# Hybrid SSD and MLA layer: attention output normalized in three calls of the chunk loop, fixed conv rows, later reciprocal and group norm, five gate buffers

## The chip, the cores and the metric

The kernel runs on one core of a Trainium2 chip. The engines named here are TensorE (PE, with its weight loads PEld), VectorE (DVE), ScalarE (ACT), GpSimd (POOL) and SyncE (SP, which here only issues DMAs). The metric is the device time of one execution in microseconds, as the median of several runs.

## What is computed

A decoder layer over a sequence of 1024 positions and 1024 channels, in float32. Two branches read the same normalized input; the gated branches are summed and go through a projection and a gated MLP.

```python
h = rms_norm(x, norm_mix_g)
z, xbc, dt_raw, q_a, kv_a, k_rope_raw, gates = split(h @ w_in)
y_ssd = ssd_mixer(z, xbc, dt_raw, ...) @ w_ssd_proj
y_mla = mla_mixer(q_a, kv_a, k_rope_raw, ...) @ w_mla_proj
g_ssd, g_mla = split(sigmoid(gates + gate_b), 2)
x = x + (g_ssd * y_ssd + g_mla * y_mla) @ w_o
u_gate, u_val = split(causal_depthwise_conv(rms_norm(x, norm_ffn_g) @ w_up, conv_ffn_w, conv_ffn_b), 2)
x = x + (silu(u_gate) * u_val) @ w_down

# ssd_mixer: 4 groups of 8 heads, state 128, chunks of 128 positions
xs, bm, cm = split(silu(causal_depthwise_conv(xbc, conv_w, conv_b)))
y = ssd_chunked_scan(xs * dt, dt * a, bm, cm) + xs * d_skip
y = rms_norm((y * silu(z)).reshape(b, l, 4, 512), norm_g)     # per group
# mla_mixer: 16 heads, causal softmax attention, output 64 wide per head
```

## The kernel before

Float32 matmuls with a wide right side are done as three passes over split operands: `split` writes a high part `hi` (on ACT) and a rest `lo` (on DVE or POOL), and `mm3` (L149 to L151) multiplies hi by hi, hi by lo and lo by hi. Weights come through `load_w`: two DMAs on SP into `wraw` (two buffers of 128 x 512), a cast to `whi` on ACT (L127), a subtraction to `wlo` on POOL (L128; `w_eng` sets the engine). A step is one such triple of 128 x 512 matmuls, and a tile of a projection takes 16 steps into the two PSUM banks `lin`.

The order on PE is the order of the code. Every other engine's order is set by the tile framework's scheduler, which simulates the program and lays instructions by when it expects them to be ready; each engine and each DMA queue then runs its own list strictly in order. A tile name with `bufs=n` is a ring of n buffers, and the next writer of a buffer waits for the last user of it, which may be a DMA that stores it.

After the attention (head sums in `l_d`, unnormalized output in `at_d`, both in HBM) the program goes on so:

1. `flush()` finishes the z gates still in the background (`z_tiles`), then the reciprocal of all head sums is made: load `l_d`, one vector instruction, store.
2. `conv_group(0)`: six tiles of `conv_tile`. Each takes 16 steps on PE, copies to a row `craw` on ACT with three zeros ahead of it (a memset on POOL for each new row), one scaled copy on ACT (L768), three shifted multiply-adds on DVE (L770), then tanh (L774) and a last product (L775) in `silu`.
3. The chunk loop over groups 0 to 3, 23 steps `u` each (`ssd_steps`): transposes `xp`, state update `sn` and `st`, outputs `yp`, gating, squares (`ssd_squares`, ACT then POOL). Between the steps `advance` puts background matmuls on PE: the next group's convolutions, z tiles, and for group 3 the MLA projection (`mla_tiles`).
4. Within it `ssd_finish` does the group norm of a half sequence: sums over partitions as matmuls by a column of ones (`np_`, L901), a reciprocal square root by bit trick and three Newton steps (twelve instructions of four columns on DVE), a broadcast of the root on PE (`np_`, L908), four products (L911) and stores to `y_d`.
5. `normalize(n)`, called every third step, 16 times with work: stores the product of the call before, loads a tile of `at_d` and, by two partition broadcasts, the reciprocals from `l_d` (both into `rb`, three buffers) and multiplies on POOL (L937).
6. `mla_tiles` for group 3: per half tile a load of the sigmoid gate from `g_d` into `rb`, 8 steps on PE, one product (L953), a store to `m_d`. Attention output is reloaded by `load_at` into `rb` or `lt` and split.

Of the kernel before, what the change touches and what calls it, by code (L numbers as in the profile page):

```python
# [72 lines left out]
def tile_hybrid_layer(ctx: ExitStack, tc: tile.TileContext, x, cols, cons, w_main, w_small, w_uq, w_ukv,  # L73
# [39 lines left out]
    def rsqrt_mean(dst, ss, n):  # L113

        w = dst.shape[1]
        v = const.tile([P, 32], F32, name="rsv", bufs=1)[:, 0:w]
        a = const.tile([P, 32], F32, name="rsa", bufs=1)[:, 0:w]
        V.tensor_scalar(v, ss, 1.0 / n, EPS, op0=ALU.mult, op1=ALU.add)
        V.tensor_scalar(dst.bitcast(I32), v.bitcast(I32), 1, None, op0=ALU.logical_shift_right)
        V.tensor_scalar(dst.bitcast(I32), dst.bitcast(I32), -1.0, float(0x5F3759DF), op0=ALU.mult, op1=ALU.add)  # L120
        for _ in range(3):
            V.scalar_tensor_tensor(a, dst, -0.5, v, op0=ALU.mult, op1=ALU.mult)
            V.tensor_tensor(a, a, dst, op=ALU.mult)
            V.scalar_tensor_tensor(dst, a, 1.5, dst, op0=ALU.add, op1=ALU.mult)

# [362 lines left out]
    with tc.tile_pool(name="cp", bufs=2) as cp, tc.tile_pool(name="pss", bufs=4, space=PSUM) as pss, \  # L488
# [235 lines left out]
        lv = l_d.rearrange("h (c t) -> (h c) t", t=P)  # L724
        ls = cp.tile([P, 512], F32, name="e", bufs=6)[:, 0:P]
        nc.sync.dma_start(out=ls, in_=lv)
        V.reciprocal(ls, ls)
        nc.sync.dma_start(out=lv, in_=ls)
# [5 lines left out]
    with tc.tile_pool(name="dp", bufs=2) as dp, tc.tile_pool(name="psx", bufs=1, space=PSUM) as psx, \  # L734
# [4 lines left out]
        abcs, zts = [], []  # L739

# [17 lines left out]
        def conv_tile(ct, c):  # L758
            w = load_w(w_main[16 + ct], [P, KD, P])
            raw = dp.tile([P, T + 3], F32, name="craw")  # L760
            G.memset(raw[:, 0:3], 0.0)
            cw = CG_CONVW + 4 * ct
            for half in range(2):
                ps = lin_tile()
                yield from steps([w], h[half], ps, range(KD), KD)
                S.copy(raw[:, 3 + half * 512:3 + half * 512 + 512], ps)
                later()
            S.activation(c, raw[:, 3:T + 3], AF.Identity, bias=col(CG_CONVB + ct), scale=col(cw + 3))  # L768
            for k in range(3):
                V.scalar_tensor_tensor(c, raw[:, k:k + T], col(cw + k), c, op0=ALU.mult, op1=ALU.add)  # L770

            def silu():
                th = raw[:, 0:T]
                S.activation(th, c, AF.Tanh, scale=0.5)  # L774
                V.scalar_tensor_tensor(c, th, 1.0, c, op0=ALU.add, op1=ALU.mult)  # L775

            pend.append(silu)
# [50 lines left out]
        def ssd_state(g, c, inp, st):  # L828
# [4 lines left out]
            nst = dp.tile([P, 512], F32, name="st", bufs=3)  # L833
# [30 lines left out]
        sums = {}  # L864

        def ssd_squares(g, c):
# [5 lines left out]
            G.tensor_tensor(sums[g, c // 4][:, (c % 4) * P:(c % 4 + 1) * P], sq[:, 0, :], sq[:, 1, :], op=ALU.add)  # L872

# [20 lines left out]
        def ssd_finish(g, half):  # L894

            x, s = chan[g], hs_(half)
            if half:
                ssd_squares(g, NT - 1)
            np_ = psy.tile([P, 512], F32, name="np_")
# [4 lines left out]
            rsqrt_mean(rr, np_[:, 0:4], 512)  # L904
            yield
# [18 lines left out]
        stores = []  # L924

        def normalize(n):

            if stores:
                nc.sync.dma_start(out=stores[0][0], in_=stores[0][1])
                stores.pop()  # L930
            if n < 16:
                k, s = n // 2, hs_(n % 2)
                raw, rb = [dp.tile([P, 512], F32, name="rb", bufs=3) for _ in range(2)]
# [3 lines left out]
                G.tensor_tensor(raw, raw, rb, op=ALU.mult)  # L937
                stores.append((at_d[k * P:(k + 1) * P, s], raw))

        def mla_tiles():  # L940
# [3 lines left out]
            def one(w, ct, half):  # L944
                s = hs_(half)
                gt = dp.tile([P, 512], F32, name="rb", bufs=3)
# [35 lines left out]
        drain([conv_group(0)])  # L982
# [4 lines left out]
        for g in range(GROUPS):  # L987
# [7 lines left out]
            for u, _ in enumerate(ssd_steps(g)):  # L995
                advance((u + 1) * n // 23 - u * n // 23)
                if u % 2 and fins and next(fins[0], 0) == 0:
                    fins.pop(0)
                if u % 3 == 1 and (g < 2 or g == 2 and u == 1):
                    normalize(8 * g + u // 3)  # L1000
                if u == 12:
# [551 lines left out]
```

## Time and profile before

| | us |
|---|---|
| median of 3 runs | 2295.05 |
| the runs | 2286.06, 2295.05, 2298.89 |
| the profiled execution | 2296.51 |
| its span, first to last instruction | 2294.4 |
| PE busy | 2205.7 |
| DVE busy | 1430.9 |
| ACT busy | 1014.1 |
| POOL busy | 755.5 |

The profiled execution is one run of the program with the trace on; its span leaves out 2.1 us at its ends. Busy times are sums over the instructions of an engine. Where an engine idles, the trace tells which event ended the idle time, read from semaphores; the engine that made the event may itself have waited. Waits are told per stretch of the span: the z gates and the first convolutions stand at about 711 to 850 us, groups 0 to 2 of the chunk loop at 850 to 1190, group 3 with the MLA projection at 1190 to 1340.

### The profile page before, as it was taken

To read this page: it belongs to the slowest core of one execution; us is meant where nothing else is said; L and a number is where in the kernel's file an instruction comes from. 1 tells how busy PE (TensorE), PEld (TensorE's weight loads), DVE (VectorE), ACT (ScalarE), POOL (GpSimd) and SP (SyncE) were. 2 spreads that over 40 slices of the span, in tenths; PEclk is the share of its full clock that TensorE was granted. 3 is DMA by queue.
4 is the path that set the end of the run, shared out by engine and by line. 5 is a ranking of instruction groups with operands and counts; after the bars stand their busy time and mean duration, and the time that the engine had idled before them with its cause. 6 is when DMAs were issued, how large, how long until landed. Compare 5 with 4: busy or idle time off the path is not lost. (4 is left out here: it accounts for less than half of the span.)

```text
span 2294.4 us, 31427 instructions
## 1 busy us (share of the span) xinstructions
PE 2205.7 (96%) x11488; PEld 1769.3 (77%) x11488; DVE 1430.9 (62%) x2496; ACT 1014.1 (44%) x1852; POOL 755.5 (33%) x821
## 2 busy tenths in 40 slices
PE   8999999999998879999998999999989999999999
PEld 7877777777776667777876778989778888888887
DVE  4566565667662348887876755645887767774432
ACT  5454454454543226565654423424544444443221
POOL 2244432444333444343423310003175555510000
PEclk9999999999999999999999999999999999999999
DMA  3111111111113542545356685543122222227541
GB/s 141 57 66 48 48 42 52 53 48 41 54 48 117 168 147 75 126 104 124 97 156 189 170 280 197 178 144 116 55 92 83 83 83 83 83 101 269 189 148 65
DMA packets 158906, 253.57 MB, mean 111 GB/s; under 512 B 13504, under 2 KB 68480, under 8 KB 158752
## 3 DMA queue, kind: packets, MB, share of 16 engines
q1 hardware_dynamic: 101232, 214.73, 27.2%
q10 hardware_dynamic: 57520, 36.84, 6.8%
q8 instruction: 90, 1.47, 0.3%
q14 instruction: 64, 0.52, 0.1%
HBM read 194.63 MB, written 56.89 MB: 110 GB/s over the span
## 5 line engine op out<-in xcount | busy, mean ns | idle before, releaser
L149 PE MATMUL lin<-h,whi 128*128 128x512 f32 x1440 | 601.1, 417 | 16.4 <-ACT whi L127 10.5
L151 PE MATMUL lin<-h,wlo 128*128 128x512 f32 x1440 | 570.2, 396 | 16.9 <-POOL wlo L128 15.9
L150 PE MATMUL lin<-h,whi 128*128 128x512 f32 x1440 | 568.2, 395 | 0.0
L149 PEld LDWEIGHTS lin<-h,whi 128*128 128x128 f32 x1440 | 274.3, 191 | 124.0 <-issue 57.0
L151 PEld LDWEIGHTS lin<-h,wlo 128*128 128x128 f32 x1440 | 273.5, 190 | 83.6 <-POOL wlo L128 21.3
L150 PEld LDWEIGHTS lin<-h,whi 128*128 128x128 f32 x1440 | 274.7, 191 | 53.7 <-issue 7.3
L127 ACT CAST whi<-wraw 128x512 fp32r<-128x512 f32 x276 | 165.3, 618 | 301.9 <-PE lin L150 118.0
L128 POOL TENSOR_TENSOR wlo<-wraw,whi 128x512 fp32r<-128x512 f32 x134 | 198.8, 1498 | 188.6 <-ACT whi L127 188.5
L621 ACT ACTIVATE e<-s 128x512 f32<-128x512 f32 (+1 forms) x192 | 93.5, 491 | 162.1 <-DVE s L619 111.2
L128 DVE TENSOR_TENSOR wlo<-wraw,whi 128x512 fp32r<-128x512 f32 x142 | 99.7, 721 | 93.2 <-ACT whi L127 93.1
L626 POOL TENSOR_TENSOR acc<-acc,e 128x512 f32<-128x512 f32 (+3 forms) x80 | 79.2, 990 | 224.1 <-ACT acc L624 134.4
L128 DVE TENSOR_TENSOR h<-ar,h 128x1024 fp32r<-128x1024 f32 x40 | 48.7, 1225 | 109.0 <-ACT h L127 108.9
L808 ACT ACTIVATE seg<-abc,acum 128x128 f32<-128x128 f32 x256 | 82.2, 390 | 41.8 <-PE yp L849 35.2
L127 ACT CAST h<-ar 128x1024 fp32r<-128x1024 f32 x40 | 42.0, 1054 | 125.8 <-PE lin L150 115.0
L770 DVE SCALAR_TENSOR_TENSOR xg<-craw,cl,xg 128x1024 f32<-128x1024 f32 x48 | 76.6, 1596 | 33.3 <-ACT xg L768 31.5
L149 PE MATMUL dps<-whi,h 128*128 128x512 f32 x240 | 93.4, 389 | 0.0
L150 PE MATMUL dps<-wlo,h 128*128 128x512 f32 x240 | 93.4, 389 | 0.0
L151 PE MATMUL dps<-whi,h 128*128 128x512 f32 x240 | 93.4, 389 | 0.0
L626 DVE TENSOR_TENSOR acc<-acc,e 128x512 f32<-128x512 f32 (+3 forms) x80 | 58.4, 730 | 48.9 <-ACT e L621 33.2
L632 PE MATMUL pv<-e,vt 128*64 128x512 f32 (+3 forms) x384 | 83.1, 513 | 0.0
L1096 POOL TENSOR_TENSOR h<-x,h 128x512 fp32r<-128x512 f32 x8 | 11.1, 1390 | 214.9 <-ACT h L1095 214.9
L1043 ACT CAST xhi<-ur 128x512 fp32r<-128x512 f32 (+1 forms) x41 | 34.0, 830 | 91.7 <-PE dps L150 86.6
(566 smaller groups left out, 5157.9 us busy)
## 6 DMA issues: line engine op xcount, KB each, us to landing
wraw<-in_w_main SPq DMA_DIRECT2D x112, 256.0 KB
ur<-in_w_up SPq DMA_DIRECT2D x44, 512.0 KB
ar<-a_d SPq DMA_DIRECT2D x40, 512.0 KB
abc<-ac_d ACTq DMA_DIRECT2D x32, 512.0 KB
wraw<-in_w_ssd SPq DMA_DIRECT2D x64, 256.0 KB
wraw<-in_w_down SPq DMA_DIRECT2D x44, 256.0 KB
a_d<-uc SPq DMA_DIRECT2D x22, 512.0 KB
g_d<-lt SPq DMA_DIRECT2D x32, 256.0 KB
```

The costliest lines, as they stand in the source:

```text
L127: S.copy(hi, raw)
L128: (eng or V).tensor_sub(lo, raw, hi.bitcast(F32))
L149: PE.matmul(ps, lhsT=ah, rhs=bh, start=first, stop=False, **more)
L150: PE.matmul(ps, lhsT=ah, rhs=bl, start=False, stop=False, **more)
L151: PE.matmul(ps, lhsT=al, rhs=bh, start=False, stop=last, **more)
L621: S.activation(e[:, c0:512], ps[:, 0:w], AF.Exp)
L626: (V if hd else G).tensor_tensor(accs[hd][:, c0:512], accs[hd][:, c0:512], e[:, c0:512], op=ALU.add)
L632: PE.matmul(pv[hd * 64:(hd + 1) * 64, c0:512], lhsT=vt[:, j, hd * 64:(hd + 1) * 64], rhs=es[hd][:, c0:512], start=first, stop=last)
L770: V.scalar_tensor_tensor(c, raw[:, k:k + T], col(cw + k), c, op0=ALU.mult, op1=ALU.add)
L808: S.activation(seg[:, hd, :], abc[:, hd, :], AF.Relu, bias=acum[:, c, 8 * g + hd:8 * g + hd + 1], scale=-1.0)
L1043: S.copy(hi, r)
L1096: eng.tensor_sub(lo, v, hi.bitcast(F32))
```

## The change

- `normalize` is now a pipeline of three calls: a call stores the product of the call before it, multiplies what the call before it loaded, and loads the next tile. The broadcast reciprocals get a ring of their own (`nb`, two buffers); `rb` keeps three. Two calls in group 2 empty the pipeline.
- `behind(name)` ties an instruction in order after another of the same engine. Each multiplication on POOL is tied after the last squares written so far, and the reciprocal after the last vector instruction at step 33 of `conv_group(0)`. The load of the sums for it is issued at step 17. Both stood at the end of the attention before.
- `craw` is two fixed rows, zeroed once; tanh writes behind the zeros.
- In `ssd_finish` the second half's squares come one step earlier, and two steps lie between the sums and the broadcast; the first half begins at step 14, no longer 12. Step 0 of a group also serves it.
- The MLA gates use `rb` (three buffers) for three of five tiles and the `chan` ring (four buffers of 1024 columns, two of them still held by the convolutions of group 3) for the other two.
- `st` has two buffers, no longer three; the scratch of `rsqrt_mean` shrinks.

```diff
+    def behind(name):
+        ins = nc.cur_bb.bb.instructions[-1]
+        if name:
+            tc.add_manual_dep(ins, name, mybir.DependencyInfo(
+                mybir.DependencyClass.NoSync, mybir.DependencyReason.DATA), reason="order")
+        return ins.name
...
-        lv = l_d.rearrange("h (c t) -> (h c) t", t=P)
-        ls = cp.tile([P, 512], F32, name="e", bufs=6)[:, 0:P]
-        nc.sync.dma_start(out=ls, in_=lv)
-        V.reciprocal(ls, ls)
-        nc.sync.dma_start(out=lv, in_=ls)
...
+        craws = [dp.tile([P, T + 3], F32, name="craw") for _ in range(2)]
+        for raw in craws:
+            G.memset(raw[:, 0:3], 0.0)
...
-            raw = dp.tile([P, T + 3], F32, name="craw")
-            G.memset(raw[:, 0:3], 0.0)
+            raw = craws[turn[0] % 2]
+            turn[0] += 1
...
-                th = raw[:, 0:T]
+                th = raw[:, 3:T + 3]
...
-            nst = dp.tile([P, 512], F32, name="st", bufs=3)
+            nst = dp.tile([P, 512], F32, name="st")
...
             G.tensor_tensor(sums[g, c // 4][:, (c % 4) * P:(c % 4 + 1) * P], sq[:, 0, :], sq[:, 1, :], op=ALU.add)
+            squared[0] = behind(None)
...
             if half:
                 ssd_squares(g, NT - 1)
+                yield
...
             rsqrt_mean(rr, np_[:, 0:4], 512)
             yield
+            yield
...
+            if loaded:
+                raw, rb, dst = loaded.pop()
+                G.tensor_tensor(raw, raw, rb, op=ALU.mult)
+                behind(squared[0])
+                stores.append((dst, raw))
             if n < 16:
                 k, s = n // 2, hs_(n % 2)
-                raw, rb = [dp.tile([P, 512], F32, name="rb", bufs=3) for _ in range(2)]
+                raw = dp.tile([P, 512], F32, name="rb", bufs=3)
+                rb = dp.tile([P, 512], F32, name="nb")
                 nc.sync.dma_start(out=raw, in_=at_d[k * P:(k + 1) * P, s])
                 for hd in range(2):
                     nc.sync.dma_start(out=rb[64 * hd:64 * hd + 64, :], in_=l_d[2 * k + hd, s].partition_broadcast(64))
-                G.tensor_tensor(raw, raw, rb, op=ALU.mult)
-                stores.append((at_d[k * P:(k + 1) * P, s], raw))
+                loaded.append((raw, rb, at_d[k * P:(k + 1) * P, s]))
...
-                gt = dp.tile([P, 512], F32, name="rb", bufs=3)
+                n = turn[0] = turn[0] + 1
+                gt = dp.tile([P, 512], F32, name="rb", bufs=3) if n % 5 < 3 else \
+                    dp.tile([P, T], F32, name="chan", bufs=4)[:, 0:512]
...
-        drain([conv_group(0)])
+        ls = dp.tile([P, P], F32, name="bt")
+        lv = l_d.rearrange("h (c t) -> (h c) t", t=P)
+        for n, _ in enumerate(conv_group(0)):
+            if n == 17:
+                nc.sync.dma_start(out=ls, in_=lv)
+            if n == 33:
+                name = [ins for ins in nc.cur_bb.bb.instructions if ins.engine == mybir.EngineType.DVE][-1].name
+                V.reciprocal(ls, ls)
+                behind(name)
+                nc.sync.dma_start(out=lv, in_=ls)
...
-                if u % 2 and fins and next(fins[0], 0) == 0:
+                if (u % 2 or u == 0) and fins and next(fins[0], 0) == 0:
                     fins.pop(0)
-                if u % 3 == 1 and (g < 2 or g == 2 and u == 1):
+                if u % 3 == 1 and (g < 2 or g == 2 and u < 5):
                     normalize(8 * g + u // 3)
-                if u == 12:
+                if u == 14:
                     fins.append(ssd_finish(g, 0))
```

The order on POOL in the first convolutions before, right after the end of the attention (`wlo<-wraw,whi` is the weight split, `rb<-rb` the normalizing product, `craw` the zeros of a conv row):

```order
L128 TENSOR_TENSOR wlo<-wraw,whi 128x512 x2
L761 MEMSET craw 128x3 x2
L937 TENSOR_TENSOR rb<-rb 128x512 x2
L128 TENSOR_TENSOR wlo<-wraw,whi 128x512 x2
L937 TENSOR_TENSOR rb<-rb 128x512
L128 TENSOR_TENSOR wlo<-wraw,whi 128x512 x2
```

And the change's POOL from the end of the attention (`acc<-acc,e` is its last work) into the chunk loop (`st`, `sq_` and `sqs` are the state step and the squares):

```order
L634 TENSOR_TENSOR acc<-acc,e 128x128
L745 MEMSET craw 128x3 x2
L136 TENSOR_TENSOR wlo<-wraw,whi 128x512 x20
L844 TENSOR_TENSOR st<-st,cdec 128x512
L879 TENSOR_TENSOR sq__8341<-sq__8341 128x256
L880 TENSOR_TENSOR sqs<-sq__8341 128x128
L945 TENSOR_TENSOR rb<-rb,nb 128x512
L136 TENSOR_TENSOR wlo<-wraw,whi 128x512 x2
```

The products have moved from between the first splits to behind the squares, one for each chunk of groups 0 and 1.

On SP the first round trips before stood among the weight loads of the first convolutions:

```order
L726 DMA e<-l_d 128x128
L728 DMA l_d<-e 128x128
L134 DMA wraw<-in_w_main 128x512
L296 DMA z_d<-lt 128x512
L134 DMA wraw<-in_w_main 128x512
L934 DMA rb<-at_d 128x512
L936 DMA rb<-l_d 64x512 x2
L934 DMA rb<-at_d 128x512
L296 DMA z_d<-lt 128x512
L929 DMA at_d<-rb 128x512
```

In the change three loads of attention output still stand there, and the store, the broadcasts (`nb`) and the reload come once per chunk, ahead of that chunk's two weight loads:

```order
L1007 DMA bt<-l_d 128x128
L952 DMA rb<-at_d 128x512 x3
L304 DMA z_d<-lt 128x512
L142 DMA wraw<-in_w_main 128x512 x2
...
L941 DMA at_d<-rb 128x512
L954 DMA nb<-l_d 64x512 x2
L952 DMA rb<-at_d 128x512
L142 DMA wraw<-in_w_main 128x512 x2
```

The round trips left the first convolutions' queue and stand in the chunk loop's, each reload two rows behind a store.

In the MLA stage SP of the change holds each gate load right behind a store (`m_d`), as before, but of another tile:

```order
L974 DMA m_d<-rb 128x512
L967 DMA rb<-g_d 128x512
L974 DMA m_d<-rb 128x512
L142 DMA wraw<-in_w_mla 128x512
L967 DMA rb<-g_d 128x512
L974 DMA m_d<-chan 128x512
L967 DMA chan<-g_d 128x512
```

The store that a load follows is that of five tiles before it.

## Rows read from the trace of the kernel before

**Rows 1.** The page, part 1: engine, busy us (share of the span) xinstructions.

```profile
span 2294.4 us, 31427 instructions
...
PE 2205.7 (96%) x11488; PEld 1769.3 (77%) x11488; DVE 1430.9 (62%) x2496; ACT 1014.1 (44%) x1852; POOL 755.5 (33%) x821
```

**Rows 2.** Windows: stretch, length, busy us (x) by engine, granted clock, DMA share, GB/s.

```profile
730.00:850.00 120.00, 93.53 (x370) 72.86 (x369) 47.57 (x33) 36.15 (x55) 54.89 (x38) 0.92 0.51 163
850.00:1190.00 340.00, 335.81 (x2058) 269.09 (x2057) 280.59 (x430) 199.07 (x373) 131.52 (x122) 1.00 0.42 110
1190.00:1300.00 110.00, 94.68 (x514) 73.44 (x513) 69.68 (x129) 52.15 (x109) 38.84 (x36) 0.92 0.64 175
```

**Rows 3.** PE's waits, 690 to 1400: who, for whom, us in total, times, longest.

```profile
PE lin L151 <- POOL wlo L128: 15.9, 9, 3.2
PE lin L149 <- ACT whi L127: 10.5, 4, 5.8
PE lin L149 <- DVE lt L294: 5.9, 2, 3.2
PE xp L798 <- DVE xg L775: 5.3, 1, 5.3
PE sn L832 <- DVE bt L822: 4.1, 2, 3.6
PE np__12351 L908 <- DVE grr L124: 3.8, 1, 3.8
PE np__8775 L901 <- POOL craw L761: 1.5, 1, 1.5
PE np__8902 L908 <- DVE grr L124: 1.1, 1, 1.1
```

**Rows 4.** Timeline of POOL, 754 to 772: start, length, instruction, idle time before it.

```profile
757.08 1.26 POOL L937 TENSOR_TENSOR rb<-rb 128x512 f32<-128x512 f32 x1 [11.77 <-DMA rb<-at_d]
758.30 2.50 POOL L128 TENSOR_TENSOR wlo<-wraw,whi 128x512 fp32r<-128x512 f32 x2
```

**Rows 5.** The tile `rb`, 690 to 860: ns min/median/max; then who waited for it.

```profile
L937 POOL TENSOR_TENSOR rb<-rb x16: 1263/1442/2325, 733.5 to 843.9; 128x512 f32<-128x512 f32 x16
...
  POOL rb L937: 73.8, 16
```

**Rows 6.** Timeline of PE, a convolution tile's steps.

```profile
748.33 0.39 PE L149 MATMUL lin<-h,whi 128*128 128x512 f32 x1
...
749.01 0.39 PE L149 MATMUL lin<-h,whi 128*128 128x512 f32 x1
```

**Rows 7.** Timeline of ACT, 728 to 850.

```profile
731.58 1.06 ACT L810 ACTIVATE seg<-seg 128x1024 f32<-128x1024 f32 x1 [3.57 <-DMA rb<-at_d]
...
836.68 0.62 ACT L127 CAST whi<-wraw 128x512 fp32r<-128x512 f32 x1 [3.77 <-DMA wraw<-in_w_main]
```

**Rows 8.** Conv steps (L770) in 730:860, then in 860:1180; splits there. ns min/median/max.

```profile
L770 DVE SCALAR_TENSOR_TENSOR xg<-craw,cl,xg x12: 1283/2180/2221, 794.5 to 843.0; 128x1024 f32<-128x1024 f32 x12
...
L770 DVE SCALAR_TENSOR_TENSOR xg<-craw,cl,xg x36: 1270/1280/2368, 901.7 to 1167.6; 128x1024 f32<-128x1024 f32 x36
...
L128 POOL TENSOR_TENSOR wlo<-wraw,whi x40: 1280/1546/2338, 869.3 to 1162.8; 128x512 fp32r<-128x512 f32 x40
```

**Rows 9.** POOL's waits, 860 to 1180.

```profile
POOL craw L761 <- DVE chan L775: 21.5, 4, 6.2
```

**Rows 10.** MLA stage, 1190 to 1300: SP's waits, then one row of ACT and DVE.

```profile
SPq L947 <- DMA m_d<-rb: 39.1, 8, 9.5
...
1225.84 0.62 ACT L127 CAST h<-lt 128x512 fp32r<-128x512 f32 x1 [9.14 <-DMA lt<-at_d]
...
1280.68 0.69 DVE L953 SCALAR_TENSOR_TENSOR rb<-rb,lin 128x512 f32<-128x512 f32 x1 [5.16 <-DMA rb<-g_d]
```

**Rows 11.** Waits in the chunk loop, 860 to 1180: SP's weight loads, ACT's weight casts.

```profile
SPq L134 <- POOL wlo L128: 217.5, 40, 18.5
...
ACT whi L127 <- DMA wraw<-in_w_main: 8.7, 3, 3.9
```

More of the change, by code (lines that the diff above doesn't have):

```diff
@@ L115, in rsqrt_mean @@
         w = dst.shape[1]
-        v = const.tile([P, 32], F32, name="rsv", bufs=1)[:, 0:w]
-        a = const.tile([P, 32], F32, name="rsa", bufs=1)[:, 0:w]
+        v = const.tile([P, 16], F32, name="rsv", bufs=1)[:, 0:w]
+        a = const.tile([P, 16], F32, name="rsa", bufs=1)[:, 0:w]
         V.tensor_scalar(v, ss, 1.0 / n, EPS, op0=ALU.mult, op1=ALU.add)
@@ L739, in tile_hybrid_layer @@
         abcs, zts = [], []
+        craws = [dp.tile([P, T + 3], F32, name="craw") for _ in range(2)]
+        for raw in craws:
+            G.memset(raw[:, 0:3], 0.0)
+        turn = [0]
         def abc_load(n):
@@ L864, in tile_hybrid_layer @@
         sums = {}
+        squared = [None]
         def ssd_squares(g, c):
@@ L922, in ssd_finish @@
             yield
-        stores = []
+        loaded, stores = [], []
         def normalize(n):
```

## The prediction

> **What bounds the kernel now.** I read four views in this order: the busy table, the windows by stage, TensorE's (PE's) waits, and then the queue each wait led to. The busy table says PE: busy 2205.7 of 2294.4 us [rows 1], so no other engine can give more than the 88.7 us in which PE sits idle, plus what a lowered clock costs. The change touches only the stretch from about 711 us (attention ends) to 1340 us. The windows show where the idle time of that stretch lies [rows 2]: 26.5 us in 730 to 850 (120.0 less 93.5), where the first group of convolutions runs and no chunk loop covers it; 4.2 us in 850 to 1190, the chunk loop over groups 0 to 2; 15.3 us in 1190 to 1300, the last group with the MLA projection. The granted clock is 0.92 in the first and third window. The two levels are 2.4 and 1.2 GHz, so 0.08 less on average means 16% of the window at the lower level: 19.2 us of 120 and 17.6 us of 110.
>
> PE's waits name the queues [rows 3]: weight splits on POOL (15.9 us in 9 waits), z gates drained late (5.9), and the first transposes of the chunk loop (5.3). These three make 27.1 us, and the window's 26.5 holds all but one short wait of them. What holds POOL is plain in its timeline [rows 4]: at 757.08 a multiplication of the attention output ends 11.8 us of waiting for its load, and the two weight splits (wlo) stand behind it, one after the other. All 16 multiplications were laid between 733.5 and 843.9, and POOL sat 73.8 us idle in front of them, waiting for loads [rows 5]. So the stage is paced by store, reload, multiply, not by PE, whose tile takes 10.9 us (16 steps of three matmuls, a step every 0.68 us [rows 6]).
>
> **The change part by part.** *Multiplications.* Load, multiply and store become three calls in the chunk loop, and each multiplication is tied behind the last squares on POOL. In the first stage POOL then has 20 splits in one run and no wait for a load in front of them. Of the 26.5 us idle the 15 us of split waits should go whole: a split pair is 2.5 us [rows 4] against 10.9 us of PE work per tile. The 5.3 us at the first transposes comes from a cast on ACT that waited 3.8 us for a weight load [rows 7] and from the vector conv steps, 2.18 us here against 1.28 us in the chunk loop [rows 8]; three of those are 2.7 us, and 3.8 and 2.7 cover 5.3. I leave 1 us. The 5.9 us of z gates stood behind an exponential on ACT that idled 3.6 us on a DMA [rows 7]; the reload of the sums and three loads of attention output still share that moment with the decay loads, so I leave half, 3. Gain 22.5 us; ends 16 (the z gates and the transposes keep everything) and 26.5.
>
> *Clock.* With PE busy 0.78 of the first window, 19.2 us at half clock cost 0.5 x 19.2 x 0.78 = 7.5 us of work. The low clock lies in the windows that have the idle time, so I let it go with the waits and leave 2. Gain 5.5; ends 0 and 7.5.
>
> *What the multiplications cost where they go.* 16 at 1.26 us, POOL's shortest [rows 5], are 20.3 us on a POOL that is busy 131.5 of 340 us [rows 2], so POOL has room. It also loses the pad memsets of `craw`, for which it waited 21.5 us [rows 9] on the vector step that frees the row; one such wait showed through as PE's 1.5 us. DVE, busy 280.6 of 340, is the tight one: a POOL operation beside it stretches both (wlo 1.28 us at best, 1.55 median, 2.34 at worst; conv steps 1.28 median, 2.37 at worst) [rows 8]. The 40 splits there live with 4.2 us of PE idle, so 16 more operations should cost 16/40 of that, 1.7; I take 2. Ends 0 and 20.3 (each multiplication holds one vector operation for its whole length, and PE waits for all of it).
>
> *Queues passed.* On SP each chunk now has a store, two broadcast loads and a reload, and the reload's buffer (`rb`, three of them) is the one whose store stands two rows ahead, so SP waits for that landing with two weight loads behind it. The nearest rows are the MLA gates, whose loads waited 39.1 us for stores in 8 waits, 4.9 us each [rows 10]. Cover: in the chunk loop SP waits 217.5 us in 40 weight loads for a free buffer [rows 11], 5.4 us each before its load may start at all, and 8.7 us of late weight loads reached ACT there without one weight wait on PE [rows 3, 11]. I take 0; without that cover it is the slower rival below. POOL's multiply comes a chunk or more after its loads, so I expect no wait for them. The state buffers fall from three to two, which ties POOL's `st` step behind the output matmuls of the chunk before; at 1 us of work I count nothing.
>
> *Group norm later.* The rank-one sums and the broadcast of the root wait on PE [rows 3]: 1.5 and 1.1 us, a second like the latter of 1.0, and 3.8. All belong to first halves, where the sums now come two steps later and the root four; the chunk loop has 69 steps in its 340 us, 4.9 us each, so 10 and 20 us against one chain of twelve small vector operations. All four go: 3.6 us in the chunk loop, 3.8 in the last group. The last was also behind a vector queue that idled 5.2 us on a gate load [rows 10], which is what the five gate buffers address.
>
> *Five gate buffers, reciprocal.* A gate load now waits for the store of five gates before, no longer three. The order shows the load still right behind the store that it needs, so SP waits as often; the gate arrives two tiles earlier. The longest late weight cast (5.8 of 10.5 us) and the 4.1 us of `sn` [rows 3] come behind reloads of attention output (9.1 us on ACT at 1225.84 [rows 10]), which nothing here moves: gain 0 there, ends 0 and 6. Clock of that window: 0.5 x 17.6 x 0.86 = 7.6 us; one of its stretches follows the 3.8 us wait, gain 1. The reciprocal (one instruction) now follows two convolution tiles, 22 us of PE work, and the first multiplication that needs it follows six: 0.
>
> **Sum.** 22.5 + 5.5 - 2 + 3.6 + 3.8 + 1 = 34.4 us. The profiled execution took 2296.5, which is 1.5 above the median of three runs (2295.05) and inside their spread; 2296.5 - 34.4 = **2262 us**.
>
> **The rivals.** (a) *Vector engine blocked in the chunk loop.* If every moved multiplication holds a two-input vector operation for its whole length and PE feels it, 20.3 us in place of 2: 2262 + 18 = 2280. For it: DVE is 83% busy and PE already waits on its `bt` and `grr` [rows 3]. Against: 40 splits do the same today at almost no price. The Trainium skill, "SBUF — State Buffer", section "Who interferes with whom", speaks for this rival: a vector instruction with both inputs in SBUF and a GpSimd instruction that reads SBUF take one port pair in turns, and the loser blocks fully. By that rule the stretching in [rows 8] is a lock, and the move costs up to those 18 us; the trace agrees that both stretch, not that PE pays.
>
> (b) *It doesn't do what it says.* POOL's splits are late because the raw weights land late (DMA share 0.51 in the window [rows 2], the cast's 3.8 us [rows 7]), and they stay late. Then the group norm's 3.6 + 3.8 is all: 2289. Against: SP's weight loads there wait in a queue that the same round trips block.
>
> (c) *Slower: the reload on SP.* Of 16 reloads 13 wait for a store with two weight loads behind each. If SP's wait outlasts the cover, a cast comes late, ACT stops behind it and PE waits; the longest PE wait of that kind is 5.8 us, and the mean 10.5/4 = 2.6 [rows 3]. At 5.8, 13 make 75 us: 2262 + 75 = 2337. It decides from six such waits (34.4/5.8); at fewer the change is still faster. Against: 217.5 us of waiting for buffers, not data.
>
> (d) *All of it:* nothing left of the 27 us, clock and `sn` included, no price: 2262 - 12 = 2250.
>
> **How the numbers follow.** Forecast 0.63; (a) 0.14, of which a quarter lies within the bound below; (b) 0.07; (c) 0.06; (d) 0.10. A measurement of this kernel tells 0.5% (11.5 us, so 2283.6) from no change. Faster: 0.63 + 0.10 + 0.11 = 0.84; within: 0.07 + 0.03 = 0.10; slower 0.06. The range runs from (d) to the upper end of (a), 2250 to 2284, which leaves out (b), (c) and a little of (a), about 0.16.
>
> **What would show it.** POOL runs its 20 splits from 712 to 830 without a load between them, and PE's waits for wlo there are under 2 us; the window that answers to 730 to 850 shows PE idle under 6 us and clock 0.97 or more. The chunk loop holds the 16 multiplications at 1.3 to 2.3 us, PE idle under 8 us there. No wait of PE on `grr`. It is wrong if PE waits for casts in the chunk loop (c), if waits for `bt`, `sn` or the output matmuls grow there to 20 us (a), or if wlo waits stay in the first stage (b).

## The result

The changed kernel takes 2276.87 us (median of 9 runs, 2270.37 to 2281.10) against 2289.51 us of the kernel before in runs beside it (9 runs, 2283.43 to 2298.89). The ratio is 0.993, with a 95% interval of 0.9915 to 0.9946: faster by 12.6 us, where 34.4 us were forecast from the profiled execution of before, which was itself 7.0 us above its own median. The profiled execution of the changed kernel took 2272.53 us, with a span of 2270.7. Both kernels were traced a second time (runs e9 and e8 below); their spans were 2284.7 and 2274.0, so one pair of traces alone tells the difference to within some 10 us.

### The profile page after: what moved, and what is told of

Its sections match the earlier page's. It is cut to its first block, busy times and chain, and to the rows that moved or that the text cites. A ratio compares the mean times of both kernels' runs of the same rounds, so it can differ in the third digit from the quotient of the medians.

```text
span 2270.7 us, 31411 instructions
## 1 busy us (share of the span) xinstructions
PE 2201.9 (97%) x11488; PEld 1769.3 (78%) x11488; DVE 1429.0 (63%) x2496; ACT 1013.8 (45%) x1852; POOL 754.8 (33%) x799
## 4 chain that ended last, share of the span: by engine, by line
PE 74%; DVE 13%; DMA 7%; ACT 4%; issue 1%; POOL 1%; SPq 1%; ACTq 0%; DVEq 0%; POOLq 0%
PE lin L157 12%; PE lin L159 11%; PE lin L158 11%; PE dps L157 8%; PE dps L158 8%; PE dps L159 8%; PE pv L640 2%; PE s L157 2%; PE s L159 2%; PE s L158 2%; PE s L597 1%; DMA rb<-at_d 1%; DMA wraw<-in_w_main 1%; DVE acc L634 1%; DVE rsa L122 1%
## 5 line engine op out<-in xcount | busy, mean ns | idle before, releaser
L136 POOL TENSOR_TENSOR wlo<-wraw,whi 128x512 fp32r<-128x512 f32 x134 | 191.3, 1445 | 244.8 <-ACT whi L135 240.3
L1126 POOL TENSOR_TENSOR h<-x,h 128x512 fp32r<-128x512 f32 x8 | 11.1, 1389 | 206.0 <-ACT h L1125 206.0
```

What stands on the lines that cost most here:

```text
L136: (eng or V).tensor_sub(lo, raw, hi.bitcast(F32))
```

## The profile after

Section 1 of the page, busy us by engine, answers to [rows 1]:

```profile
PE 2201.9 (97%) x11488; PEld 1769.3 (78%) x11488; DVE 1429.0 (63%) x2496; ACT 1013.8 (45%) x1852; POOL 754.8 (33%) x799
```

The work is the same but for 22 short memsets on POOL; idle time and clock moved. The windows that answer to [rows 2] (stretch, length, busy us and instructions of PE, PEld, DVE, ACT and POOL, granted clock, DMA share, GB/s), each cut at the matmuls that stood at the ends of the windows before:

```profile
732.70:815.30 82.60, 82.60 (x369) 68.50 (x368) 36.66 (x32) 29.34 (x41) 18.77 (x15) 1.00 0.25 80
815.30:1163.40 348.10, 339.43 (x2058) 270.48 (x2057) 292.20 (x429) 198.29 (x375) 165.88 (x122) 0.99 0.54 142
1163.40:1273.30 109.90, 94.93 (x513) 73.73 (x513) 69.71 (x128) 50.67 (x104) 40.76 (x35) 0.92 0.70 184
```

The matmuls of the first window take 82.6 us instead of 120, with no idle time on PE; a wait of 1.9 us for a z gate stands just ahead of it. Those of the chunk loop take 348.1 us instead of 340, with 8.7 us of idle time instead of 4.2. The last group is as idle as before (15.0 us) at the same clock. PE's waits from 700 to 1400, which answer to [rows 3] (who, for whom, us in total, times, longest):

```profile
PE sn L839 <- DVE bt L829: 17.3, 6, 8.6
PE lin L159 <- DVE wlo L136: 5.0, 1, 5.0
PE lin L157 <- ACT whi L135: 2.3, 2, 1.5
PE lin L157 <- DVE lt L302: 1.9, 1, 1.9
PE lin L159 <- POOL wlo L136: 1.4, 2, 0.8
```

The 15.9 us of splits on POOL have become 1.4, late casts 2.3 instead of 10.5, and no row on `grr` is left. In their place stand the state matmuls, which wait for `bt` (17.3 instead of 4.1; 6.1 of it in the chunk loop, 11.2 in the last group), and one wait of 5.0 us on a split on DVE, at the start of the last projection. POOL in the first stage (a group of instructions: busy us, mean ns, idle time before them) and the moved multiplications (ns min/median/max, first and last start) answer to [rows 4] and [rows 5]:

```profile
L136 POOL TENSOR_TENSOR wlo<-wraw,whi 128x512 fp32r<-128x512 f32 x20 | 25.7, 1307 | 85.1 <-ACT whi L135 85.1
...
L945 POOL TENSOR_TENSOR rb<-rb,nb x16: 1270/1299/2327, 830.8 to 1047.6; 128x512 f32<-128x512 f32 x16
```

Twenty splits with no load between them, each pair waiting for its cast alone, and 16 multiplications at 1.27 to 2.33 us between 830.8 and 1047.6: the change does what it says.

To see where the time went, I measure by work: the chunk loop has 28 state matmuls (`sn`), and their starts on PE divide the program. For the changed kernel, from PE's timeline, the first, fifth, fourteenth, twenty-first and last:

```profile
817.36 1.11 PE L839 MATMUL sn<-xde,bt 128*128 128x512 f32 x2
...
869.32 1.02 PE L839 MATMUL sn<-xde,bt 128*128 128x512 f32 x2
...
1017.67 0.59 PE L839 MATMUL sn<-xde,bt 128*128 128x512 f32 x1
...
1140.84 0.59 PE L839 MATMUL sn<-xde,bt 128*128 128x512 f32 x1
...
1279.74 0.59 PE L839 MATMUL sn<-xde,bt 128*128 128x512 f32 x1
```

The kernel before has them at 853.18, 905.02, 1047.18, 1169.10 and 1308.48, and 848.54 to 1298.22 in its second trace. The attention's last value matmul is loaded at 705.6 and 702.7 before, 704.3 and 704.1 after. So, in us, both traces of each:

| stretch | before | after | forecast gain | measured gain (means) |
|---|---|---|---|---|
| attention to sn 1 (first stage) | 147.6, 145.8 | 113.1, 112.0 | 28 | 34.2 |
| sn 1 to 5 | 51.8, 51.8 | 52.0, 52.0 | 0 | -0.2 |
| sn 5 to 14 | 142.2, 142.1 | 148.4, 148.4 | 1.6 with the next | -6.2 |
| sn 14 to 21 | 121.9, 121.9 | 123.2, 123.1 | | -1.3 |
| sn 21 to 28 (last group) | 139.4, 133.8 | 138.9, 139.1 | 4.8 | -2.4 |
| sn 28 to the end (tail) | 985.9, 986.5 | 991.0, 995.3 | 0 | -6.9 |

The work between the marks is the same but for eight short matmuls of the group norm (1.1 us), which move from before sn 14 to behind it, and from before sn 28 into the tail. The rows add up to a gain of 17.2 us, 4.6 more than the medians show, since the two traced executions of the changed kernel lie below its median and those of before on the whole above theirs. The first stage gained more than forecast; 17 us were given back behind it. The experiments ask by what. All medians below are to be read against some 2288 us of the kernel before in the same study (2288.09, 2288.23, 2287.56 and 2287.88 in the four).

## The experiments

**The move undone (e1).** The changed kernel with the old one-call `normalize`:

```diff
+                raw, rb = [dp.tile([P, 512], F32, name="rb", bufs=3) for _ in range(2)]
...
+                G.tensor_tensor(raw, raw, rb, op=ALU.mult)
+                stores.append((at_d[k * P:(k + 1) * P, s], raw))
-                loaded.append((raw, rb, at_d[k * P:(k + 1) * P, s]))
```

> The changed kernel with one part undone: the attention output is normalized in one call as before (load, multiplication, store in one go, both tiles from the three rb buffers), everything else of the change stays. My theory: the gain is the first stage, and it comes from the 16 multiplications leaving POOL there. Then the 16 multiplications stand between 733 and 845 us again, PE waits for wlo there for 12 us or more, the first transposes (xp) come at about 840 us instead of 813.8, and the time is that of the kernel before or a little less (2285 to 2290 us, ratio 0.998 to 1.00), because the later group norm gives back some 3 us. Rival: the gain is carried by the other parts (group norm, reciprocal, pad rows, gate buffers); then this kernel is as fast as the changed one, about 2277 us (ratio 0.993).

2286.48 us, ratio 0.999 (0.9975 to 1.0004): the gain is gone, as expected. But not in the expected place. The transposes came at 810.8 us, as early as in the changed kernel; the first multiplication now starts at 771.9, since the reciprocal is laid later, and the series of 16 runs into the chunk loop. There POOL waits again for the loads, with two splits behind (timeline of POOL, and PE's waits from 700 to 910):

```profile
856.21 1.26 POOL L948 TENSOR_TENSOR rb<-rb 128x512 f32<-128x512 f32 x1 [9.77 <-DMA rb<-l_d]
857.43 2.49 POOL L136 TENSOR_TENSOR wlo<-wraw,whi 128x512 fp32r<-128x512 f32 x2
...
PE lin L159 <- POOL wlo L136: 12.8, 3, 10.4
```

From sn 1 to 5 this kernel takes 67.5 us instead of 52. So the loss sticks to POOL's waiting multiplications wherever they stand, and the later reciprocal alone only shifts it.

**The move alone (e2).** The kernel before with the new `normalize` and `behind`, two state buffers and the narrower root scratch that make room:

```diff
-                raw, rb = [dp.tile([P, 512], F32, name="rb", bufs=3) for _ in range(2)]
+                raw = dp.tile([P, 512], F32, name="rb", bufs=3)
+                rb = dp.tile([P, 512], F32, name="nb")
...
+                G.tensor_tensor(raw, raw, rb, op=ALU.mult)
+                behind(squared[0])
```

> The kernel before with one part of the change alone: the three-step normalization, each multiplication tied behind the last squares (two state buffers, and the two root scratch tiles cut to 16 columns, to make room). My theory: the first stage gains as in the changed kernel, so xp starts at 814 to 818 us, and the chunk loop loses some 7 us or more as it does there; time 2277 to 2282 us (ratio 0.994 to 0.997), the lack of the later group norm costing 3 us. Rival: the other parts are needed for the first stage (the reciprocal and its reload still stand ahead of the casts, the pad memsets still wait): xp at 830 us or later and 2288 us or more.

2265.58 us, ratio 0.9917 (0.9887 to 0.9948), `xp` at 813.9. The move carries all of the gain, and this kernel is below both expectations: 22.5 us under before, where the whole change made 12.6. Its last group takes 133.8 us and its tail 988.8, 5 and some 4 us less than in the changed kernel. So some other part of the change costs time.

**Multiplications without trips, and the reverse (e3, e4).** e3 leaves the multiplication out, e4 the loads and stores:

```diff
-                G.tensor_tensor(raw, raw, rb, op=ALU.mult)
-                behind(squared[0])
```

> The changed kernel with the 16 multiplications left out (the attention output stays unnormalized): loads and stores of the three steps all stay, POOL has 21 us less to do in the chunk loop. Theory A (vector engine slowed by POOL): PE's 17.3 us of waits for bt and the longer chunks of group 1 (15 to 17 us between sn matmuls where the kernel before has 13 to 14) go away, time about 2277 - 12 = 2265 us. Theory B (the round trips delay transfers, and ACT stands behind them): the waits for bt stay above 10 us and the time stays within 4 us of 2277.

```diff
-                nc.sync.dma_start(out=raw, in_=at_d[k * P:(k + 1) * P, s])
...
+                G.tensor_tensor(nbs[0], nbs[0], nbs[1], op=ALU.mult)
+                behind(squared[0])
```

> The changed kernel with the loads and stores of the attention output and of the sums left out (so it stays unnormalized); 16 multiplications of the same size stay on POOL, on two resident tiles, tied behind the squares as in the changed kernel. Theory A (vector engine slowed by POOL): waits for bt stay near 17 us and the time stays within 4 us of 2277. Theory B (round trips): bt waits fall under 6 us, no wait of ACT in the chunk loop ends on a landing of attention output, time about 2265 us.

2273.87 us (0.9947, 0.9929 to 0.9965) and 2270.49 us (0.993, 0.9909 to 0.9951). e3 answered another question than it was asked. With no multiplication there is no tie behind the squares, and the scheduler laid all 16 trips into the first stage (stores from SP, first and last start):

```profile
L941 SPq DMA_DIRECT2D at_d<-rb x16: 319/320/727, 724.7 to 772.7; - x16
```

That stage then took 126.0 us instead of 113, so the trips alone, without POOL, cost 13 us of the 34 there (PE waits 11.1 us in it for z gates, 1.9 in the changed kernel). But it leaves a chunk loop with neither trips nor multiplications, e4 one with multiplications alone, and the changed kernel one with both. The windows from sn 5 to sn 14 of e3, of e4 and of the changed kernel (columns as above):

```profile
883.10:1021.50 138.40, 136.69 (x853) 109.41 (x852) 123.89 (x191) 87.71 (x168) 64.45 (x48) 1.00 0.43 113
```

```profile
868.20:1012.10 143.90, 137.29 (x852) 109.34 (x851) 131.67 (x193) 87.52 (x168) 78.92 (x58) 1.00 0.43 108
```

```profile
869.30:1017.70 148.40, 140.78 (x853) 111.26 (x852) 130.80 (x192) 86.98 (x168) 78.82 (x58) 0.98 0.62 160
```

Without both, 138.4 us: 3.8 under the 142.2 of before, of which 1.1 is the work that moved behind the mark, so the group norm and the fixed conv rows gain 2.7 here where 3.6 were forecast. Ten multiplications add 14.5 us to POOL's busy time and 7.8 to DVE's, and PE takes 5.5 us longer, 4.9 of them idle. Two more vector instructions fall into e4's window (a convolution step and a short one, some 2 us), so the same instructions take some 6 us longer. Most of that, 4.8 us, is in the smallest ones: the 27 instructions of four columns of the Newton steps take 6.3 us in e3, 11.1 in e4 and 9.7 in the changed kernel. A multiplication tied behind the squares runs right beside them. DVE, then POOL of the changed kernel, from their timelines:

```profile
1010.50 1.21 DVE L122 SCALAR_TENSOR_TENSOR rsa<-grr,rsv 128x4 f32<-128x4 f32 x1
...
1010.41 1.28 POOL L945 TENSOR_TENSOR rb<-rb,nb 128x512 f32<-128x512 f32 x1
```

An instruction that takes 0.16 us alone (the median of its line in e3) starts 0.09 us behind the multiplication and ends 0.02 us behind it, after 1.21 us.

The trips add 4.5 us more, at the same busy time of DVE. Of these only 1.0 is idle time; 3.5 is longer busy time of PE, at a granted clock of 0.98 instead of 1.00. In the second trace (e8) the same 148.4 us hold 9.0 us of idle time at 0.99, so how the 4.5 divide changes with the execution. Theory A and theory B each hold about half; the scheduler laid both kernels out anew, so the halves are approximate. The waits for `bt` that theory A was to be read from (13.6 us without multiplications, 18.4 without trips) don't tell, since some 12 of each stand in the last group.

**The parts of the rest (e5, e6, e7) and a second trace (e8).** e5 takes back the later group norm (the two added yields are gone too), e6 the gates outside `rb`, e7 both:

```diff
-                if (u % 2 or u == 0) and fins and next(fins[0], 0) == 0:
+                if u % 2 and fins and next(fins[0], 0) == 0:
...
-                if u == 14:
+                if u == 12:
```

> The changed kernel with the group norm laid as in the kernel before (first half queued at step 12, one yield fewer at each of the two places, called on odd steps only). The move alone (previous study) was 11 us below the changed kernel, so some other part costs that much. Theory F (the later group norm lays its vector steps into the first chunks of the next group, where the vector engine is tight): the 120.8 us between the seventh and the fourteenth sn matmul fall to 114 us or less, and the time is 2268 us or less, even though PE waits for grr again by some 3 us. Theory G (the gate buffers cost it, at the start of the MLA stage): time 2275 to 2281 us, the step from sn 21 to sn 22 stays at 45 us.

```diff
-                gt = dp.tile([P, 512], F32, name="rb", bufs=3) if n % 5 < 3 else \
-                    dp.tile([P, T], F32, name="chan", bufs=4)[:, 0:512]
+                gt = dp.tile([P, 512], F32, name="rb", bufs=3)
```

> The changed kernel with the MLA gates in the three rb buffers as before. Theory G: the 45.2 us from sn 21 to sn 22 fall to 40 us and the time to 2270 us or less. Theory F: the same 45 us, and the last chunks lose some us to late gates; time 2276 to 2282 us.

> The changed kernel with both of these undone: what is left is the move, the fixed rows for the convolutions, and the later reciprocal. If the later group norm and the gate buffers are what costs (F, G or both), it comes to the move alone, 2266 us (2262 to 2270). If the fixed rows or the later reciprocal cost it, it stays at 2275 us or more.

> The changed kernel once more, unaltered, beside the others on the same chip, for a second trace. If the losses read from its first trace belong to the kernel, they stand here again: xp from 812 to 816 us, waits for bt of 14 us or more in the chunk loop, the longest of them at the start of the MLA stage, a wait for wlo of some 5 us in the first tile of the last projection; time 2272 to 2281 us.

| | us (runs) | ratio, interval | sn 5 to 14 | 14 to 21 | 21 to 28 | tail |
|---|---|---|---|---|---|---|
| e8, the change again | 2275.98 (4) | 0.9945, 0.9928 to 0.9961 | 148.4 | 123.1 | 139.1 | 995.3 |
| e5, old group norm | 2267.17 (4) | 0.9907, 0.9889 to 0.9925 | 146.7 | 126.4 | 136.7 | 989.1 |
| e6, three gate buffers | 2269.65 (5) | 0.9933, 0.9909 to 0.9956 | 148.6 | 123.2 | 132.4 | 992.0 |
| e7, both | 2273.41 (4) | 0.9934, 0.9914 to 0.9954 | 146.8 | 126.5 | 137.5 | 988.4 |
| e2, the move alone | 2265.58 (5) | 0.9917, 0.9887 to 0.9948 | 146.8 | 124.0 | 133.8 | 988.8 |

e8 repeats its first trace: the same stretches to 0.2 us from sn 1 to sn 28, `xp` at 812.5, 19.3 us of waits for `bt`, a 4.7 us wait for `wlo` in the tail. e5 is the fastest form of the changed kernel, 9 us below it, with an interval wholly below that of e8; no interval of these overlaps the 1.00 of before. With the later group norm three gate buffers have a median 6 us better, with the old one 6 us worse, but in both pairs the intervals overlap, so no effect of the gate buffers is shown. e7 lies between the two bounds that were set for it and decides nothing about the fixed rows and the later reciprocal. Theory F is half right: sn 7 to 14 fell from 120.8 to 113.8 us in e5 and the time to 2267, but sn 5 to 6 rose by 5.4, where PE waits again 1.9 us for the sums of squares and 0.6 for the root; and e10 to e12 below show another reason for part of the 7 us. Theory G fell: the step from sn 21 to sn 22 took 44.4 us in e6, not 40.

That step goes with the group norm instead: 38.3 to 40.4 us in the five traces with the old one (before twice, e2, e5, e7), 43.3 to 47.9 in the nine with the later one in any form, whatever the gate buffers. From sn 22 to 28 it is the other way, 94.0 to 101.1 us and 88.0 to 93.8, so the last group loses some 6 us by it and gains some 5.

The tail separates as cleanly: it is 985.9 to 989.1 us in the same five traces and 991.0 to 995.5 in the nine. Of these 6 us 1.1 is the moved work, and 3.5 in the mean are idle time of PE (17.4 to 18.9 us in the five, 985.9 - 967.0 = 18.9 in the first of before; 19.8 to 23.9 in the nine, 19.8 and 21.0 in the two of the changed kernel). The rest, some 1.4 us, is longer busy time; the granted clock is its likely place (1.00 at the shortest busy time, 0.99 at the others), which was not tested. A new wait of PE for a split (`wlo`) on DVE, 2.8 to 6.1 us at the start of the last projection, stands in all nine. In the changed kernel a product on DVE (L1155) waits there for a reload of the MLA branch (`mt`). Before, one `wlo` stands ahead of that product; in the changed kernel both stand behind it:

```
1613 L128 TENSOR_TENSOR wlo<-wraw,whi 128x512
1614 L1124 SCALAR_TENSOR_TENSOR gt<-gt,lin 128x512
1615 L128 TENSOR_TENSOR wlo<-wraw,whi 128x512
1616 L1125 TENSOR_TENSOR gt<-gt,mt 128x512
```

```
1618 L1154 SCALAR_TENSOR_TENSOR gt<-gt,lin 128x512
1619 L1155 TENSOR_TENSOR gt<-gt,mt 128x512
1620 L136 TENSOR_TENSOR wlo<-wraw,whi 128x512 x2
```

Timeline of DVE and then of PE in the changed kernel, 1326 to 1330:

```profile
1328.49 0.69 DVE L1155 TENSOR_TENSOR gt<-gt,mt 128x512 f32<-128x512 f32 x1 [1.19 <-DMA mt<-m_d]
1329.10 1.28 DVE L136 TENSOR_TENSOR wlo<-wraw,whi 128x512 fp32r<-128x512 f32 x2
...
1329.84 0.79 PE L159 MATMUL lin<-h,wlo 128*128 128x512 f32 x1 [4.99 <-DVE wlo L136]
```

and of DVE in e5, where the second split runs ahead and PE's waits for `wlo` there are 1.1 us at most (it waits 2.8 us for a cast instead, as before does 3.0):

```profile
1318.89 0.69 DVE L136 TENSOR_TENSOR wlo<-wraw,whi 128x512 fp32r<-128x512 f32 x1
1320.17 0.69 DVE L1153 TENSOR_TENSOR gt<-gt,mt 128x512 f32<-128x512 f32 x1 [0.59 <-DMA mt<-m_d]
```

**Before again (e9).** The kernel before, unaltered.

> The kernel before once more, unaltered, for a second trace: the profiled execution of before took 7 us more than the median of its runs (2296.5 against 2289.5). If that is scatter from one execution to the next, this ratio is 1.00, and the second trace shows the same waits in the same places (wlo 14 us or more and xp at 838 to 846 us in the first stage, 142 us from sn 5 to sn 14) with a span nearer 2286; the difference then lies in the stretches of lower clock and in single late transfers.

2289.22 us, ratio 1.0004 (0.9993 to 1.0015), span 2284.7 where the first trace had 2294.4. PE's waits from 690 to 1400, in part:

```profile
PE lin L151 <- POOL wlo L128: 13.8, 9, 3.5
...
PE np__8902 L908 <- DVE grr L124: 1.1, 1, 1.1
PE np__10011 L908 <- DVE grr L124: 1.0, 1, 1.0
...
PE np__12753 L908 <- DVE grr L124: 0.2, 1, 0.2
```

The splits (13.8 us) and `xp` (835.1 us) came a little under what was expected; the waits in the chunk loop are the same to a tenth. The 3.8 us of `np__12351` in the last group [rows 3] are not there, and that group takes 133.8 us instead of 139.4. It was the scatter of one execution. A wait of such length (3.0 us on `grr` in the last group) stands in one more trace with the old group norm, e7, and in none with the later one.

**First halves late only (e10, e11).** From the two halves of theory F, a version that keeps the delay where it paid, with five and with three gate buffers:

```diff
-                yield
...
-            yield
+            if not half:
+                yield
...
-                if (u % 2 or u == 0) and fins and next(fins[0], 0) == 0:
+                if u % 2 and fins and next(fins[0], 0) == 0:
```

> The changed kernel with only the first halves of the group norm laid later (queued at step 14, two yields before the broadcast); the second halves, which end in the next group's first chunks, are laid as in the kernel before. Theory F, refined: the first halves' delay is worth 5.4 us at sn 6 (14.2 against 19.6) and 3 us at sn 13, the second halves' delay costs the 7 to 10 us between sn 7 and sn 14 and some 3 to 6 us in the tail (wlo behind a gate's load). Then sn 6 comes after 14.2 us, sn 7 to 14 take 114 us or less, and the time is some 5 us below the old finish (2267.2), 2262 us (2258 to 2266). Rival: any shift of these steps only moves the waits to other chunks; 2265 to 2272 us.

> The same with the gates in the three rb buffers. With the later second halves three buffers were 6 us better than five (2269.7 against 2276), with the old finish 6 us worse (2273.4 against 2267.2). If the number of gate buffers has an effect of its own, it shows here with the sign of one of these; if it only re-deals the order of loads at the start of the MLA stage, this lands within 4 us of the run with five.

2272.50 us (0.9917, 0.989 to 0.9944) and 2272.15 us (0.9928, 0.9906 to 0.995). sn 6 came after 14.2 us, but sn 7 to 14 took 120.2 and 117.2: the refined theory fell, and the gate buffers have no sign of their own here. What e10, e11, e6, e8 and the changed kernel share, and e2, e5, e7 and e4 don't, is a stop of ACT in group 1. In the changed kernel the chain of waits runs through it, from the decay load (`abc`) on (start, us, what):

```profile
907.78 9.95 DMA abc<-ac_d
...
917.74 2.34 POOL rb L945
...
920.10 3.73 DMA at_d<-rb
...
923.85 10.43 DMA rb<-at_d
...
934.30 0.37 ACTq L761
...
934.72 1.06 ACT seg L817
...
936.76 1.23 DVE abc L832
```

A multiplication is stored, the store frees the buffer, the reload into it takes 10.4 us, and only when it has landed does ACT go on. ACT does not use that data. It stands at the issue of a z-gate load (L761), which is in its own stream:

```
897 L815 ACTIVATE seg_9359<-abc_9238,acum_87 128x128
898 L761 DMA zt_9399<-z_d_76 128x4x128 [waits DMAHW6_49]
899 L817 ACTIVATE seg_9359<-seg_9359 128x1024 [waits Activation_49]
```

In the built program the transfers take eight semaphores in turn, in the order of the whole program, and one waits at its issue for the transfer eight places before. For this load that is the reload in all five kernels with the stop (8.4 to 10.5 us), and in e2 and e5 a weight load that had landed.

**The z loads on SP (e12).**

```diff
-                nc.scalar.dma_start(out=t, in_=z_d[4 * g * P:4 * (g + 1) * P, c * P:(c + 1) * P]
+                nc.sync.dma_start(out=t, in_=z_d[4 * g * P:4 * (g + 1) * P, c * P:(c + 1) * P]
```

> The changed kernel with one word altered: the loads of the z gates (zt from z_d), one per chunk, are issued from SP's queue and no longer from ACT's. Theory S: the 8.6 us in group 1 are ACT standing at such a load until the reload of attention output that was issued eight transfers before it has landed, because the two use the same one of eight transfer semaphores; with the load out of ACT's stream, no wait of ACT ahead of an exponential ends on that reload, the stretch from sn 7 to sn 14 falls from 120.8 us to 114 us or less, and the time from 2276 to 2268 us (2264 to 2271). Rival P (POOL beside the vector engine sets the pace there): the stretch stays at 118 us or more and the time within 3 us of 2276. Rival Q (SP stands instead, and weight loads behind it come late): PE waits for whi or wlo in the chunk loop by 5 us or more, time 2276 us or more.

2275.70 us, ratio 0.9952 (0.9936 to 0.9968). No wait of ACT in group 1 ends on a reload of attention output any more, and DVE waits there for ACT's `abc` 4.2 us instead of 10.4: the mechanism is shown. Its price is smaller than theory S had it. sn 5 to 14 takes 145.0 us instead of 148.4, sn 7 to 14 117.4 instead of 120.8, between the two bounds. The 3.4 us were lost again ahead of the loop, where PE waited 6.7 us in one piece for a z gate. PE's waits in the window from sn 5 to 14:

```profile
PE sn L839 <- DVE bt L829: 3.4, 2, 3.2
PE lin L157 <- DVE lt L302: 1.5, 1, 1.5
PE yp L856 <- DVE seg L818: 1.0, 1, 1.0
```

## Why the prediction was right, and where it was not

The direction and the reason hold: the gain is the first stage, and it comes from the multiplications leaving POOL there (e1, e2), with the trips that fed them: these alone would have kept 13 of its 34 us (e3). The time lies within 2250 to 2284, but in part by luck: the gain was forecast at 34.4 us and measured at 12.6, and 7.0 of the 21.8 us between them are hidden by a base that was 7.0 too high. From the median of nine runs the same sum gives 2255 and a range of 2243 to 2277, with the measured 2276.87 at its very end. By the steps of the prediction:

- *Base.* The sum was made against 2296.5 us, 7.0 above the median of nine runs. The median of three runs gave no hint of it, but their spread of 12.8 us did; e9 shows the scatter.
- *First stage and clock, 28 us.* Measured 34.2. Of the three reserves that were left (transposes 1, z gates 3, clock 2 us) only the z gates kept anything, 1.9 us; the splits kept nothing, as forecast, and the granted clock of the window is 1.00 where 0.97 was the test. All tests named for this stage came out.
- *Multiplications in the chunk loop, 2 us within 0 to 20.3.* This is the term that was mis-sized. It costs 10.0 us from sn 5 to 14 (148.4 against 138.4 in e3) and 1.8 from there to sn 21 (123.2 against 121.4): 5.5 of the 10.0 by POOL beside DVE, 4.5 by the trips, which the prediction had at 0. The argument by which 40 splits live there with 4.2 us of idle time was a false scale: 16 more operations cost 11.8 us in all. That the first 40 use up the slack is the likely reason, not a shown one. Rival (a) had 2280, nearer to the result than the forecast, and its mechanism is one half of the price, though its sign, waits of 20 us in the loop, did not come (6.1 us for `bt`): for 14.5 us of POOL the same vector instructions took some 6 us longer, and PE 5.5. The Trainium skill, "SBUF — State Buffer", section "Who interferes with whom", has the shared port pair as an exclusive lock, for a vector instruction with two inputs in SBUF beside a GpSimd instruction that reads SBUF. The trace agrees for the single instruction, held to the end of the multiplication at 1011.69; by that rule all 14.5 us could have been added to DVE (an estimate of the most), and some 6 were. PE idle in the loop came to 8.7 us against the "under 8" named.
- *Queues passed, 0 us.* SP did stand for the stores in 13 reloads, the number of rival (c), but only 26.0 us in all, 2.0 each where the MLA gates had 4.9 (rows below); it stood longer, 113.4 us, for the multiplications whose product it stores. PE waited for no weight in the loop, as forecast. The wait fell on a queue that the prediction did not look at: ACT's, which issues loads too. In e12 it was worth 3.4 us.
- *Group norm, 3.6 us in the chunk loop.* 2.7 (e3 against before, with the fixed rows), and no wait on `grr` is left there. Its side effects, some 5 us in the tail and 6 at the start of the last group, were not seen. As a whole the term has the wrong sign in this kernel: taking the later group norm back made it 8.8 us faster (e5 against e8; with three gate buffers, e7 against e6, no difference is shown).
- *Last group, 3.8 + 1 us.* The 3.8 us wait is absent in the second trace of before, so there was little to gain. The clock did not rise either (0.92). What the changed kernel has more in the last group than that trace (5.3 us) begins with 8.6 us for `bt` at 1186; the chain of waits ahead of it runs over a load of attention output (9.55 us) and a weight load (6.39). The step that holds it goes with the later group norm and not with the five gate buffers: it takes 44.4 us in e6 with three of them, and 39.4 in e7. How the later group norm brings it about stays open.
- *Rivals (b), (c), (d).* (b) fell with the first stage. (c) needed six long waits for casts; there are two, of 1.5 us at most. (d) left no price behind, and there was one of 17 us.

SP's two waits in the chunk loop, 815 to 1163 (for whom, us in total, times, longest), then the two rows of that chain in the last group (start, us, what):

```profile
SPq L941 <- POOL rb L945: 113.4, 15, 13.1
...
SPq L952 <- DMA at_d<-rb: 26.0, 13, 6.3
```

```profile
1153.79 9.55 DMA rb<-at_d
...
1175.74 6.39 DMA wraw<-in_w_mla
```

Best of all measured: the move alone (2265.58 us) and the changed kernel with the old group norm (2267.17); their intervals overlap.

## What to carry to other kernels

Work that waits for data was gained in full here when it left the stage that it held up, but it has to be priced where it lands by the slack that is left there, not by the price of similar work that already runs in that slack. A load issued from a compute engine's own stream stops that engine for whatever the load waits for, a shared semaphore included: look at every queue that issues, not at SP's alone. A wait that stands in one trace is no gain until a second execution shows it, and a base taken from one execution carries that execution's scatter into the forecast.

## What the runs showed of the hardware

Ten multiplications on POOL (14.5 us) lengthen the same vector instructions by some 6 us in 140 (e3, e4), most of it in instructions of four columns: one of 0.16 us took 1.21 beside a multiplication of 1.28. A 256 KB reload took 10.4 us from issue to landing at a DMA share of 0.62, in a loop where the kernel before moved 0.44. And two executions of one program differ by 4.3 us in the tail (991.0 and 995.3), with PE's waits there within 1.1 us (16.1 and 17.2 in sum) and a granted clock of 0.96 and 0.94 in the 120 us from 1579 and 1578: a difference of a few us in one trace needs no cause in the code.
